# Adding the passes of an FFN projection onto x1's rows by DMA, under a stricter rule for fetching activation blocks

## The chip, the cores and the metric

The kernel runs on one core of a Trainium2 chip. The metric is the device time of one execution in microseconds (us).

## What is computed

One layer of a hybrid decoder on x of 512 tokens by 2048 features, in float32. Cut to what matters here:

```
h   = RMSNorm(x);  proj = h @ W_in                       # u, v_sgu, q, k, v_att, g_a, g_b
x1  = x  + (sigmoid(g_a) * (y_a @ W_up_a) + sigmoid(g_b) * (y_b @ W_up_b)) @ W_o
hid = silu(gate) * up,   [gate | up] = RMSNorm(x1) @ W_ffn_in       # 5632 wide
x2  = x1 + hid @ W_ffn_out                               # this product is the place of the change
out = x2 + sigmoid(RMSNorm(x2) @ W_pg) * (p @ W_ple)
```

y_a is a chunked spatial gating of u and v_sgu, y_b a stick-breaking attention. Activations lie transposed: features on the 128 partitions, tokens along the free axis. A block of 128 x 1024 holds two tiles of 128 features for all 512 tokens.

## The kernel before, in words

**Products.** Every float32 operand is split into a high part (ACT, a rounding copy to fp32r) and a low part (DVE, the difference), and a product is the sum of three matmuls (L284 to L286: high by high, high by low, low by high; L695 where two of them go as one). A unit is one 256 x 256 block of weights by one activation block. A unit of kind "S" goes by Strassen's seven products and needs seven blocks for each side; one of kind "P" goes plainly with four. The strings PASSES, GATE and OUT give each unit's kind.

**Weights.** SP loads a unit's weights (L327 plain; L329 and L331 for "S"). For "S", a DMA on POOL's queue then adds two blocks onto two others on the way (L351, accum_op=add), DVE adds two more sums (L363), ACT writes the high parts whi (L347) and DVE the low parts wlo (L344).

**Forms.** The activation side of a unit is a "form" in the SBUF arena `parts`, built from raw blocks in the arena `wholes` (128 x 13312 float32). A form of kind "S" is built in two halves: its block is loaded (L504), ACT and DVE split it (L274, L275) and the unit can be used plainly at once; later the block is loaded a second time with room for the Strassen sums, L513 forms these (after the gains of a norm, L508, where there are any), and L274 and L275 split them. `PLAIN_UNTIL` and `GATE_UNTIL` say for how many outputs of a stage a unit is still taken plainly while its second half is made.

**The clock that sets the order.** The program is written out in the order of a counter. After every few products `tick()` advances it by one; there are two ticks to an "S" pair of units. At each tick: (1) of the first three forms waiting in `builds` (AHEAD = 3), the first whose source has been written and for which there is room gets its block fetched; (2) the first form whose block was fetched WAIT = 2 ticks ago takes its first building step, or else one form of the queue `seconds` has its second block fetched; (3) what was put off by `after(n, ...)` and is due is issued. Every arena gives out its places by age: "old" takes the place that was given back the longest ago. What a tick issues is tied to its place among the matmuls on every engine.

**The stages.** In FFN-in, 44 outputs of hid are made and stored to DRAM as 22 blocks. The product with W_ffn_out runs over these 22 units in three passes of 8, 8 and 6 units, with eight outputs of 128 x 1024 each (`pair`, then `out` or `onto`):

- pass 0: each output is stored as a row block of `sum` (L1436, SP);
- pass 1: `sum` is loaded (L504), the output added onto it (L804 for outputs mixed from Strassen products, L808 for plain ones), and it is stored again (L1441);
- pass 2: `sum` and the row block of x1 are loaded, the output is added (L804), the whole is scaled by the norm's row (L1224), x1 is added (L1444), x2 stored (L1445), and its squares go to the third norm (L956, L960).

The scaling comes last because the norm's factor is one number for each token and so commutes with the product. The gate stage then builds its forms from the stored x2 rows with gains (L508) and finishes each output (L1455 on). Forms of the next stage are appended to `builds` before the last output of a stage, those of the gate stage before pass 2 begins.

Of the kernel before, what the change touches and what calls it, by code (L numbers as in the profile page):

```python
# [37 lines left out]

AHEAD, WAIT = 3, 2
PARTS = 16 * PLACE + 1024  # L40
# [27 lines left out]
def hybrid_layer(  # L68
# [44 lines left out]
    class Arena:  # L113
        def __init__(self, name, n, dt):
            self.tile, self.dt = keep.tile([P, n], dt, name=name), dt
            self.holes = [(0, n)]
            self.given, self.turns = np.zeros(n // P, int), 0

        def take(self, n, how="low"):


            spots = []
            for start, size in self.holes:
                end = start + size
# [10 lines left out]
            at = min(spots)[1]  # L135
            start, size = next(h for h in self.holes if h[0] <= at < h[0] + h[1])
            self.holes.remove((start, size))
            self.holes.extend(
                h for h in ((start, at - start), (at + n, start + size - at - n)) if h[1])
            return Block(self, at, n)  # L140

        def give(self, block):
            self.turns += 1
            self.given[block.start // P : -(-(block.start + block.n) // P)] = self.turns
            holes = sorted(self.holes + [(block.start, block.n)])
            self.holes = holes[:1]
            for s, n in holes[1:]:
# [40 lines left out]
    newest = {}  # L188
    builds, seconds = deque(), deque()

# [9 lines left out]
    def tick():  # L200

        clock[0] += 1
        last, units = traced()[-1], dict(newest)
        urgent = [f for f in seconds if f.used]
        sizes = []
        for f in list(builds)[: 0 if urgent else AHEAD]:
            sizes += [s for s in f.sizes if s[0] is parts]
            raw = [(wholes, 1024, "old")]
# [224 lines left out]
    class Form(Staged):  # L433


        def __init__(self, kind, steps, sizes, ready, src=None, far=False):
# [3 lines left out]
            self.src, self.there, self.block, self.due = src, not far, None, 0  # L440
            self.second, self.due_second, self.forced = None, 0, False

# [854 lines left out]
    ys = {(c, i): y_form(c, i) for c in "ba" for i in range(4)}  # L1297
    builds.extend(ys.values())
    for n, ((w, i), pr) in enumerate(zip(order, made())):
# [24 lines left out]
        else:  # L1324
# [9 lines left out]
          for j, k in enumerate(OUT) for how in [{} if k == "S" else {"how": "high"}]]  # L1334
    builds.extend(ms)
    for j in range(KU):
        for b in "ba":
# [14 lines left out]
            else:  # L1352
# [7 lines left out]
    norm2 = Norm()  # L1360
    spill = {(n, j): tc.dram_tile([P, 1024], F32, name=nm(n)) for n in ("x1", "sum", "x2")
             for j in range(KU)}
# [9 lines left out]
    for j in range(KU):  # L1372
        if j < KU - 1:
            raw.append(load(xT[j + 1]))
        if j == 1:
            ple_operands()
            builds.extend(fs)
        pr = pair(ms, last=j == KU - 1)
# [31 lines left out]
    for m in range(KH):  # L1410
        if m == KH - 1:
            builds.extend(hs[0])
        o = pair(fs, last=m == KH - 1, j=m, until=(1,) * KU, doubled=7).out()
# [10 lines left out]
    for c, units in enumerate(hs):  # L1424
        first, at = at, at + len(units)
        if c == len(hs) - 1:
            builds.extend(gs)
        for j in range(KU):
            if j == KU - 1 and c < len(hs) - 1:
                builds.extend(hs[c + 1])  # L1430
            before = load(spill["sum", j]) if c else None
            x1 = load(spill["x1", j]) if c == len(PASSES) - 1 else None
            pr = pair(units, last=j == KU - 1, j=j, until=PLAIN_UNTIL[c], at=first,
                      doubled=7)
            if before is None:
                nc.sync.dma_start(out=spill["sum", j], in_=pr.out())  # L1436
                continue
            h = before.f()
            pr.onto(h)
            if x1 is None:  # L1440
                nc.sync.dma_start(out=spill["sum", j], in_=h)  # L1441
            else:
                scaled(h, row2)
                nc.vector.tensor_tensor(out=h, in0=h, in1=x1.f(), op=ALU.add)  # L1444
# [122 lines left out]
```

## Time and profile before

| what | value |
|---|---|
| time, three executions | 2689.34, 2690.93, 2696.23 us; median 2690.93 |
| the profiled execution, its own time | 2691.74 us |
| its span in the trace | 2690.0 us |
| mean granted clock of TensorE | 0.998 |
| busy: PE, PEld, DVE, ACT, POOL | 2653.3, 2325.7, 2207.7, 1388.7, 458.2 us |
| pass 0 | 2058.0 to 2212.5 us of the span |
| pass 1 | 2212.5 to 2375.3 |
| pass 2 | 2375.3 to 2509.2 |
| gate stage | 2509.2 to 2690.0 |

PE is the TensorE matmul queue, PEld its weight loads, DVE VectorE, ACT ScalarE, POOL GpSimd and SP SyncE, which issues DMAs. L351 is line 351 of the kernel before. A row of PE's timeline gives the start, the length, the instruction, and in brackets how long the engine stood before it and what ended that. The span is what the trace covers of an execution, its own time is a little longer; the predicted time is set against the median.

### The profile page before, as it was taken

The page shows a single profiled execution, that of the slowest core. Times are in us where ns is not written, and L with a number is a line of the kernel's source. Part 1 is how long each engine was busy: PE and PEld are TensorE (multiplying, and loading weights), DVE is VectorE, ACT ScalarE, POOL GpSimd, SP SyncE. Part 2 cuts the span into 40 slices and gives each one's busy share as a digit, 9 for nine tenths or more (in the row PEclk, how much of TensorE's full clock was granted, in tenths as well). Part 3 has the DMA queues.
Part 4 walks back from the last instruction along what each step waited for, and adds up shares of the span by engine and source line. Part 5 has one row for each costly group of instructions (what it writes and reads, how often), then busy time and mean ns, then how long its engine had stood idle before and what let it go on. Part 6 is the DMA issues. An engine that isn't in the chain of part 4 may idle for free.

```text
span 2690.0 us, 42553 instructions
## 1 busy us (share of the span) xinstructions
PE 2653.3 (99%) x15496; PEld 2325.7 (86%) x15496; DVE 2207.7 (82%) x3715; ACT 1388.7 (52%) x2161; POOL 458.2 (17%) x549
## 2 busy tenths in 40 slices
PE   8999999999999999999999999999999999999999
PEld 7889898889898889988888888888888888888898
DVE  8687878787887666688898888888899889889876
ACT  7656565655554334375444444444445444444543
POOL 0223323232220000001111111111110111100010
PEclk9999999999999999999999999999999999999999
DMA  7677777777776457667888888888888979978884
GB/s 226 154 185 175 182 173 184 172 183 198 174 187 196 140 164 211 178 210 198 230 212 213 204 202 200 201 206 199 207 197 244 259 213 279 259 254 259 257 248 126
DMA packets 288241, 548.62 MB, mean 204 GB/s; under 512 B 25888, under 2 KB 138272, under 8 KB 288032
## 3 DMA queue, kind: packets, MB, share of 16 engines
q1 hardware_dynamic: 229232, 441.03, 50.3%
q0 software_dynamic: 58800, 104.88, 25.2%
q8 instruction: 121, 1.98, 0.3%
q14 instruction: 88, 0.72, 0.1%
HBM read 498.63 MB, written 47.19 MB: 203 GB/s over the span
## 4 chain that ended last, share of the span: by engine, by line
PE 85%; DVE 7%; DMA 3%; ACT 2%; issue 2%; POOL 1%; SPq 0%; DVEq 0%; ACTq 0%; POOLq 0%
PE ps L695 47%; PE ps L285 10%; PE ps L286 10%; PE ps L284 10%; PE small L695 6%; DVE wlo L344 2%; DVE out L754 1%; DMA wholes<-x 1%; DVE parts L275 1%; PE small L1157 1%; DMA wholes<-hid 1%; DVE wholes L363 1%; ACT whi L347 1%; DVE wholes L513 1%; PE small L1032 1%
## 5 line engine op out<-in xcount | busy, mean ns | idle before, releaser
L695 PE MATMUL ps<-parts,whi 128*128 128x512 f32 x3960 | 1324.8, 397 | 0.3 <-DVE p L754 0.3
L347 ACT ACTIVATE whi<-wholes 128x512 fp32r<-128x512 f32 (+3 forms) x933 | 866.0, 942 | 787.0 <-DVE wholes L363 274.0
L344 DVE TENSOR_TENSOR wlo<-wholes,whi 128x512 fp32r<-128x512 f32 (+3 forms) x933 | 974.1, 1078 | 85.6 <-ACT whi L347 85.4
L695 PEld LDWEIGHTS ps<-parts,wlo 128*128 128x128 f32 x3960 | 743.7, 188 | 168.1 <-issue 1.0
L695 PE MATMUL ps<-parts,wlo 128*128 128x256 f32 x3960 | 784.3, 279 | 0.1
L285 PE MATMUL ps<-parts,whi 128*128 128x256 f32 (+1 forms) x2070 | 679.5, 329 | 4.8 <-DVE parts L275 4.7
L284 PE MATMUL ps<-parts,whi 128*128 128x256 f32 (+1 forms) x2048 | 668.1, 328 | 12.4 <-ACT parts L274 10.6
L286 PE MATMUL ps<-parts,wlo 128*128 128x256 f32 (+1 forms) x2070 | 677.6, 329 | 1.7 <-DVE wlo L344 1.7
L695 PEld LDWEIGHTS ps<-parts,whi 128*128 128x128 f32 x3960 | 637.8, 189 | 5.9 <-issue 1.0
L285 PEld LDWEIGHTS ps<-parts,whi 128*128 128x128 f32 x2070 | 393.6, 190 | 46.5 <-DVE parts L275 7.3
L284 PEld LDWEIGHTS ps<-parts,whi 128*128 128x128 f32 x2048 | 388.5, 190 | 48.9 <-ACT parts L274 12.7
L286 PEld LDWEIGHTS ps<-parts,wlo 128*128 128x128 f32 x2070 | 393.5, 190 | 36.2 <-DVE wlo L344 3.2
L363 DVE TENSOR_TENSOR wholes<-wholes 128x256 f32<-128x256 f32 (+1 forms) x806 | 338.9, 420 | 19.1 <-issue 1.7
L754 DVE TENSOR_TENSOR out<-out,ps 128x256 f32<-128x256 f32 x460 | 190.8, 417 | 150.9 <-ACT out L751 150.2
L351 POOL DMA_DIRECT2D wholes<-w_ffn_in x172 | 150.1, 872 | 689.1 <-DVE wholes L363 251.7
L351 POOL DMA_DIRECT2D wholes<-w_in x132 | 118.3, 898 | 484.4 <-DMA wholes<-w_in 133.7
L695 PE MATMUL small<-parts,whi 128*128 128x512 f32 x440 | 174.5, 397 | 0.0
L275 DVE TENSOR_TENSOR parts<-wholes,parts 128x1024 fp32r<-128x1024 f32 (+4 forms) x134 | 131.0, 989 | 17.6 <-ACT parts L274 17.6
L274 ACT ACTIVATE parts<-wholes 128x1024 fp32r<-128x1024 f32 (+4 forms) x134 | 112.9, 865 | 46.9 <-DVE wholes L513 26.1
L351 POOL DMA_DIRECT2D wholes<-w_ffn_out x64 | 55.8, 872 | 402.5 <-DMA wholes<-w_ffn_out 101.6
L751 ACT ACTIVATE out<-ps 128x256 f32<-128x256 f32 x243 | 91.4, 385 | 47.5 <-PE ps L695 44.0
L1403 ACT ACTIVATE out<-out 128x512 f32<-128x512 f32 x44 | 27.9, 633 | 156.3 <-DVE out L1402 156.3
(120 smaller groups left out, 1721.6 us busy)
## 6 DMA issues: line engine op xcount, KB each, us to landing
wholes<-w_ffn_in SPq DMA_DIRECT2D x172, 384.0 KB, 5.6
wholes<-w_in SPq DMA_DIRECT2D x132, 384.0 KB, 5.0
wholes<-w_ffn_in SPq DMA_DIRECT2D x172, 256.0 KB, 4.8
wholes<-w_ffn_in POOLq DMA_DIRECT2D x172, 256.0 KB, 5.5
wholes<-w_in SPq DMA_DIRECT2D x132, 256.0 KB, 4.2
wholes<-w_in POOLq DMA_DIRECT2D x132, 256.0 KB, 4.9
wholes<-w_ffn_out SPq DMA_DIRECT2D x64, 384.0 KB, 5.4
wholes<-hid SPq DMA_DIRECT2D x42, 512.0 KB, 5.8
```

Of the source, the lines that this page charges most:

```text
L274: return (nc.scalar.activation(hi, src, AF.Copy), nc.vector.tensor_tensor(out=lo, in0=src, in1=hi.bitcast(F32), op=ALU.subtract))
L275: nc.vector.tensor_tensor(out=lo, in0=src, in1=hi.bitcast(F32), op=ALU.subtract))
L284: nc.tensor.matmul(ps, sh, mh, start=start, stop=False)
L285: nc.tensor.matmul(ps, sh, ml, start=False, stop=False)
L286: return nc.tensor.matmul(ps, sl, mh, start=False, stop=stop)
L344: in_turn(nc.vector.tensor_tensor(out=self.lo[:, blocks], in0=r, in1=h.bitcast(F32), op=ALU.subtract))
L347: in_turn(nc.scalar.activation(h, r, AF.Copy))
L351: nc.gpsimd.dma_start(out=raw[:, 3:5], in_=self.src[:, 1:3], accum_op=ALU.add)
L363: in_turn(nc.vector.tensor_tensor(out=o, in0=x, in1=y, op=ALU.add))
L695: m = nc.tensor.matmul(out, l, r, start=first and k == 0, stop=last and k == 1)
L751: in_turn(nc.scalar.activation(out, x, AF.Copy, scale=scale))
L754: in_turn(nc.vector.tensor_tensor(out=out, in0=x, in1=y, op=op))
```

## The change

Three things change; everything up to the last output of FFN-in is issued as before. Lines of helpers move down by 17 (L504 becomes L521, L351 becomes L368, L513 becomes L530).

- Each pass's output is scaled by the norm's row at once (24 times instead of 8). Passes 0 and 1 put off, by two ticks, a DMA on POOL's queue that adds the output onto x1's row block in DRAM. The tensor `sum` with its 16 stores and 16 loads is gone. Pass 2 loads only x1's row block, adds its output, and stores x2 one tick later.
- A block is fetched only into a place of `wholes` that was given back at least REST = 2 ticks ago (`rested`). The same holds for second halves.
- Forms carry the number of their stage; while a form of an earlier stage still waits for its second block, no block of a later stage is fetched.

```diff
-AHEAD, WAIT = 3, 2
+AHEAD, WAIT, REST = 3, 2, 2
@@ Arena
-            self.given, self.turns = np.zeros(n // P, int), 0
-
-        def take(self, n, how="low"):
+            self.given, self.when = np.zeros(n // P, int), [0]
+
+        def spots(self, n, how):
             spots = []
...
+            return spots
+
+        def rested(self, n):
+            spots = self.spots(n, "old")
+            return bool(spots) and clock[0] - self.when[min(spots)[0]] >= REST
+
+        def take(self, n, how="low"):
+            at = min(self.spots(n, how))[1]
...
         def give(self, block):
-            self.turns += 1
-            self.given[block.start // P : -(-(block.start + block.n) // P)] = self.turns
+            self.given[block.start // P : -(-(block.start + block.n) // P)] = len(self.when)
+            self.when.append(clock[0])
@@ tick
+        stage = min((f.stage for f in seconds), default=1 << 30)
         sizes = []
         for f in list(builds)[: 0 if urgent else AHEAD]:
+            if f.stage > stage or not wholes.rested(1024):
+                break
             sizes += [s for s in f.sizes if s[0] is parts]
...
-        elif seconds and fits([(wholes, 5 * 256, "old")]):
+        elif seconds and fits([(wholes, 5 * 256, "old")]) and wholes.rested(5 * 256):
             (urgent or seconds)[0].fetch_second()
@@ the three passes
-            before = load(spill["sum", j]) if c else None
-            x1 = load(spill["x1", j]) if c == len(PASSES) - 1 else None
+            end = c == len(hs) - 1
+            h = load(spill["x1", j]) if end else None
             pr = pair(units, last=j == KU - 1, j=j, until=PLAIN_UNTIL[c], at=first,
                       doubled=7)
-            if before is None:
-                nc.sync.dma_start(out=spill["sum", j], in_=pr.out())
+            o = pr.out()
+            scaled(o, row2)
+            if not end:
+                after(2, lambda o=o, j=j: nc.gpsimd.dma_start(
+                    out=spill["x1", j], in_=o, accum_op=ALU.add))
                 continue
-            h = before.f()
-            pr.onto(h)
-            if x1 is None:
-                nc.sync.dma_start(out=spill["sum", j], in_=h)
-            else:
-                scaled(h, row2)
-                nc.vector.tensor_tensor(out=h, in0=h, in1=x1.f(), op=ALU.add)
-                nc.sync.dma_start(out=spill["x2", j], in_=h)
+            nc.vector.tensor_tensor(out=h.f(), in0=h.f(), in1=o, op=ALU.add)
+            norm3.add(h)
+
+            def store(h=h, j=j):
+                nc.sync.dma_start(out=spill["x2", j], in_=h.f())
                 there.add(("x2", j))
-                norm3.add(before)
-                give(x1)
-            give(before)
+                give(h)
+
+            after(1, store)
```

Each list of forms gets its stage number by `build(forms)`, which takes the place of `builds.extend(forms)`. On POOL's queue, 64 accumulates of w_ffn_out stand in a row before; afterwards the 16 accumulates onto x1 stand among them, one after every one to five.

**The first place** is on SP, at the step from pass 0 to pass 1. The hid rows are the activation blocks; those of pass 1 are numbered 10836 to 10843 in the kernel before. The sum rows belong to outputs, w_ffn_out to weights.

```order
L504 DMA wholes<-hid_10836 128x1024
L329 DMA wholes<-w_ffn_out 128x2x256
L331 DMA wholes<-w_ffn_out 128x768
L504 DMA wholes<-sum_9218 128x1024
L329 DMA wholes<-w_ffn_out 128x2x256
L331 DMA wholes<-w_ffn_out 128x768
L1436 DMA sum_9225<-out_20054 128x1024
L327 DMA wholes<-w_ffn_out 128x1024
L504 DMA wholes<-hid_10842 128x1024
L504 DMA wholes<-hid_10837 128x1024
L327 DMA wholes<-w_ffn_out 128x1024
L504 DMA wholes<-hid_10843 128x1024
```

The same place after the change, where the blocks of pass 1 are numbered 10828 to 10835:

```order
L346 DMA wholes<-w_ffn_out 128x2x256
L348 DMA wholes<-w_ffn_out 128x768
L521 DMA wholes<-hid_10834 128x1024
L521 DMA wholes<-hid_10835 128x1024
L521 DMA wholes<-hid_10828 128x1024
L346 DMA wholes<-w_ffn_out 128x2x256
L348 DMA wholes<-w_ffn_out 128x768
L344 DMA wholes<-w_ffn_out 128x1024
L521 DMA wholes<-hid_10829 128x1024
L344 DMA wholes<-w_ffn_out 128x1024
L521 DMA wholes<-hid_10830 128x1024
L521 DMA wholes<-hid_10831 128x1024
```

The seventh and eighth first blocks (10842 and 10843 before, 10834 and 10835 after) stood behind second halves and a sum load and store; now they stand ahead of every second half.

**The second place** is on SP, at the step from pass 1 to pass 2, whose blocks are 10844 to 10849 before. First the kernel before:

```order
L504 DMA wholes<-hid_10847 128x1024
L327 DMA wholes<-w_ffn_out 128x1024 x2
L504 DMA wholes<-hid_10848 128x1024
L504 DMA wholes<-sum_9218 128x1024
L327 DMA wholes<-w_ffn_out 128x1024
L329 DMA wholes<-w_ffn_out 128x2x256
L331 DMA wholes<-w_ffn_out 128x768
L504 DMA wholes<-x_823_9210 128x1024
L1441 DMA sum_9225<-wholes 128x1024
L329 DMA wholes<-w_ffn_out 128x2x256
L331 DMA wholes<-w_ffn_out 128x768
L504 DMA wholes<-hid_10849 128x1024
```

After the change, with blocks 10836 to 10841 in pass 2 (x_823 and x_824 are x1's first two row blocks):

```order
L344 DMA wholes<-w_ffn_out 128x1024 x5
L521 DMA wholes<-hid_10840 128x1024
L521 DMA wholes<-x_823_9210 128x1024
L344 DMA wholes<-w_ffn_out 128x1024
L346 DMA wholes<-w_ffn_out 128x2x256
L348 DMA wholes<-w_ffn_out 128x768
L521 DMA wholes<-hid_10841 128x1024
L521 DMA wholes<-hid_10837 128x1024
L521 DMA wholes<-x_824_9211 128x1024
L346 DMA wholes<-w_ffn_out 128x2x256
L348 DMA wholes<-w_ffn_out 128x768
L521 DMA wholes<-hid_10838 128x1024
```

The first blocks of units 1 to 4 (10836 to 10839) are no longer here: they stand early in pass 1, with the second block of the first unit. The sum rows are gone.

**The third place** is on DVE at the same step, in the last output of pass 1, just ahead of the split of the first second half. Before:

```order
L754 TENSOR_TENSOR p_1786_21489<-p_1786_21489,ps_21389 128x256
L754 TENSOR_TENSOR out_21484<-out_21484,ps_21395 128x256
L754 TENSOR_TENSOR out_21484<-out_21484,p_1786_21489 128x2x256
L754 TENSOR_TENSOR out_21484<-out_21484,ps_21395 128x256
L754 TENSOR_TENSOR out_21484<-ps_21400,out_21484 128x256
L754 TENSOR_TENSOR out_21484<-small_21405,out_21484 128x256
L754 TENSOR_TENSOR out_21484<-out_21484,ps_21400 128x256
L754 TENSOR_TENSOR out_21484<-out_21484,small_21405 128x256
L344 TENSOR_TENSOR wlo_79<-wholes,whi_78 128x1024
L275 TENSOR_TENSOR parts<-wholes,parts 128x4x256
```

After:

```order
L530 TENSOR_TENSOR wholes<-wholes 128x256 x3
L771 TENSOR_TENSOR out_21476<-out_21476,ps_21385 128x256
L530 TENSOR_TENSOR wholes<-wholes 128x256
L771 TENSOR_TENSOR out_21476<-out_21476,p_1802_21481 128x2x256
L771 TENSOR_TENSOR out_21476<-out_21476,ps_21385 128x256
L771 TENSOR_TENSOR out_21476<-ps_21390,out_21476 128x256
L771 TENSOR_TENSOR out_21476<-small_21395,out_21476 128x256
L771 TENSOR_TENSOR out_21476<-out_21476,ps_21390 128x256
L771 TENSOR_TENSOR out_21476<-out_21476,small_21395 128x256
L361 TENSOR_TENSOR wlo_79<-wholes,whi_78 128x1024
L292 TENSOR_TENSOR parts<-wholes,parts 128x4x256
```

Four additions of the first unit's Strassen sums (L530) now stand among the mixing of the output (L771, L754 before), ahead of the split.

More of the change, by code (lines that the diff above doesn't have):

```diff
@@ L134, in take @@
                                      for a in {*range(start, end - n + 1, 256), end - n})
-            at = min(spots)[1]
+            return spots
[4 more added lines that the diff above has]
+            at = min(self.spots(n, how))[1]
             start, size = next(h for h in self.holes if h[0] <= at < h[0] + h[1])
@@ L188, in hybrid_layer, with build @@
     newest = {}
-    builds, seconds = deque(), deque()
+    builds, seconds, stages = deque(), deque(), iter(range(1 << 30))
+    def build(forms):
+        stage = next(stages)
+        for f in forms:
+            f.stage = stage
+        builds.extend(forms)
     def mark(instruction):
@@ L440, in __init__ @@
             self.src, self.there, self.block, self.due = src, not far, None, 0
-            self.second, self.due_second, self.forced = None, 0, False
+            self.second, self.due_second, self.forced, self.stage = None, 0, False, -1
         def fetch(self):
@@ L1297, in hybrid_layer @@
     ys = {(c, i): y_form(c, i) for c in "ba" for i in range(4)}
-    builds.extend(ys.values())
+    build(ys.values())
     for n, ((w, i), pr) in enumerate(zip(order, made())):
@@ L1334, in hybrid_layer @@
           for j, k in enumerate(OUT) for how in [{} if k == "S" else {"how": "high"}]]
-    builds.extend(ms)
+    build(ms)
     for j in range(KU):
@@ L1360, in hybrid_layer @@
     norm2 = Norm()
-    spill = {(n, j): tc.dram_tile([P, 1024], F32, name=nm(n)) for n in ("x1", "sum", "x2")
+    spill = {(n, j): tc.dram_tile([P, 1024], F32, name=nm(n)) for n in ("x1", "x2")
              for j in range(KU)}
@@ L1376, in hybrid_layer @@
             ple_operands()
-            builds.extend(fs)
+            build(fs)
         pr = pair(ms, last=j == KU - 1)
@@ L1411, in hybrid_layer @@
         if m == KH - 1:
-            builds.extend(hs[0])
+            build(hs[0])
         o = pair(fs, last=m == KH - 1, j=m, until=(1,) * KU, doubled=7).out()
```

4 lines of the change are left out of this document (2 added, 2 removed).

## The prediction

> **What bounds the kernel now.** I read first the page's busy times and the chain that ended last, then the four stages that the change can reach (pass 0, pass 1, pass 2 and the gate stage) as four windows, then PE's waits in them, and last the instructions ahead of each wait.
>
> ```profile
> span 2690.0 us, 42553 instructions
> PE 2653.3 (99%) x15496; PEld 2325.7 (86%) x15496; DVE 2207.7 (82%) x3715; ACT 1388.7 (52%) x2161; POOL 458.2 (17%) x549
> PE 85%; DVE 7%; DMA 3%; ACT 2%; issue 2%; POOL 1%; SPq 0%; DVEq 0%; ACTq 0%; POOLq 0%
> ```
>
> PE is busy for 99% of the span and holds 85% of the chain. Its matmuls are the same 15378 program rows before and after, so a gain can only come out of the time in which PE stands or runs slowly. The stages, with the columns window, length, PE, PEld, DVE, ACT, POOL, PE's clock, DMA share, GB/s:
>
> ```profile
> 2058.00:2212.50 154.50, 154.49 (x876) 134.43 (x875) 136.67 (x238) 77.94 (x104) 21.82 (x25) 1.00 0.86 248
> 2212.50:2375.30 162.80, 160.85 (x902) 139.40 (x901) 148.15 (x252) 78.81 (x105) 21.80 (x25) 1.00 0.90 263
> 2375.30:2509.20 133.90, 127.31 (x790) 114.38 (x789) 116.06 (x169) 61.47 (x77) 10.47 (x12) 0.99 0.83 258
> 2509.20:2690.00 180.80, 172.75 (x1097) 157.40 (x1095) 134.29 (x205) 81.88 (x109) 19.93 (x20) 0.99 0.71 209
> ```
>
> Pass 0 has no PE idle time to win; pass 1 has 1.95 us, pass 2 6.59, and the gate stage 8.05 (the kernel's tail with its last stores among it). PE's timeline names each pause: start, length, and in brackets the idle time before and its releaser.
>
> ```profile
> 2228.89 0.50 PE L285 MATMUL ps<-parts,whi 128*128 128x512 f32 x1 [1.25 <-DVE parts L275]
> 2242.52 0.62 PE L284 MATMUL ps<-parts,whi 128*128 128x256 f32 x3 [0.64 <-ACT parts L274]
> 2390.92 0.73 PE L284 MATMUL ps<-parts,whi 128*128 128x512 f32 x2 [1.52 <-ACT parts L274]
> 2419.66 0.62 PE L284 MATMUL ps<-parts,whi 128*128 128x256 f32 x3 [2.04 <-ACT parts L274]
> 2421.31 0.39 PE L285 MATMUL ps<-parts,whi 128*128 128x256 f32 x1 [0.32 <-DVE parts L275]
> 2423.33 0.62 PE L284 MATMUL ps<-parts,whi 128*128 128x256 f32 x3 [1.05 <-ACT parts L274]
> 2424.59 0.39 PE L285 MATMUL ps<-parts,whi 128*128 128x256 f32 x1 [0.64 <-DVE parts L275]
> 2463.22 0.39 PE L286 MATMUL ps<-parts,wlo 128*128 128x256 f32 x1 [1.02 <-DVE wlo L344]
> 2528.03 0.80 PE L944 MATMUL small<-diag,ones 128*128 128x128 f32 x4 [0.76 <-DVE diag L942]
> 2564.13 0.39 PE L285 MATMUL ps<-parts,whi 128*128 128x256 f32 x1 [2.00 <-DVE parts L275]
> ```
>
> Together 11.24 us. Eight of the ten wait for L274 or L275, the split of a form: the first products of a stage wait for an activation block that was fetched or split late. Two windows in which the clock fell follow right behind the largest groups of them:
>
> ```profile
> 2425.30:2428.70 3.40, 3.40 (x15) 3.11 (x14) 2.91 (x5) 3.10 (x5) 0.00 (x0) 0.50 0.90 336
> 2565.30:2568.70 3.40, 3.40 (x18) 3.40 (x17) 3.40 (x4) 0.26 (x1) 0.00 (x0) 0.50 0.82 243
> ```
>
> Half a clock for 3.40 us loses 1.7 us, so 3.4 us in both. No more than 11.24 + 3.4 = 14.6 us can be won, 0.5%.
>
> Here a rule of the Trainium skill can be weighed. Its page "TensorE: Matmul & The Clock Gate", section "HAM oscillation — how this bites in real kernels", says that PE must not idle for more than about 3.4 us; by it pauses of 2.0 us would leave the clock alone, and the 3.4 us would stay whatever becomes of them. The trace does not agree: the longest single pause before either window is 2.04 or 2.00 us.
>
> **What the change costs and brings, part by part.** *Where the forms are fetched* (first and second place of the order). Before, SP issued the blocks of the next stage among sum loads and stores, and one of them was seen to hold ACT up:
>
> ```profile
> 2215.39 2.47 SPq L504 DMA_DIRECT2D wholes<-hid  x2
> 2219.87 1.46 SPq L504 DMA_DIRECT2D wholes<-hid  x2
> 2389.81 1.06 ACT L274 ACTIVATE parts<-wholes 128x1024 fp32r<-128x1024 f32 x1 [3.11 <-DMA wholes<-hid]
> ```
>
> In pass 1 the first of each of those SP pairs is the seventh and the eighth block of the stage; they came 13.5 and 9.0 us before the pause at 2228.89. In the changed order they stand 53 to 60 matmuls earlier, ahead of every second half; a matmul of that stage is 160.85/902 = 0.18 us, so some 10 us. The 1.25 us go. In pass 2 the first blocks of units 1 to 4 are fetched early in pass 1, and of the stage's end only units 5 and 6, the second halves and two x1 rows are left; the sum loads that stood between are gone. I take the five pauses from 2390.92 to 2424.59 away: 1.52 + 2.04 + 0.32 + 1.05 + 0.64 = 5.57 us, and the clock window behind them, 1.7. In the gate stage the late block's split is now ordered 76 matmuls ahead of its reader: 2.00 and 1.7 us go. The pause of 0.64 stays, since the second half of pass 1's second form is again split about ten matmuls ahead of its use; I add another 0.64 for the same pattern one form earlier. The 0.76 us stay: L942 is not touched.
>
> *DVE.* What its operations take:
>
> ```profile
> L804 DVE TENSOR_TENSOR wholes<-wholes,out 128x1024 f32<-128x1024 f32 x13 | 15.9, 1220 | 0.0
> L1224 DVE TENSOR_TENSOR wholes<-wholes 128x1024 f32<-128x1024 f32 x8 | 9.8, 1220 | 0.1
> L1444 DVE TENSOR_TENSOR wholes<-wholes 128x1024 f32<-128x1024 f32 x8 | 9.8, 1222 | 0.1
> L513 DVE TENSOR_TENSOR wholes<-wholes 128x256 f32<-128x256 f32 x78 | 30.9, 419 | 5.3 <-ACT wholes L508 2.8 <-DMA wholes<-hid 2.3
> ```
>
> Pass 0 gains eight scalings, 8 x 1.22 = 9.8 us: DVE goes from 136.67 to about 146 of 154.5. Its cover is that pass 1 already runs at 148.15 of 162.8 with the same count of such operations for each output, and no pause of it comes from wlo or from the mixing of outputs. I count 0; without that cover it would be at most 9.8. Pass 1 trades an addition for a scaling: 0. Pass 2 loses eight operations of 1.22 us. There the pause of 1.02 us at 2463.22 came when L344 stood behind L804, L1224 and L1444 of one pair, 3.7 us; with 1.2 us less in the row it goes. The new cost stands at the third place of the order: four additions (30.9/78 = 0.40 us each, 1.6 together) now go ahead of a split that PE reads one matmul later. PE waits between 0 and the largest pause of the kind, 2.0; I take 1.0, the middle, which is near the 1.25 and 1.05 above.
>
> *The new store of x2, one tick later.* A tick here is 2.8 us (133.9 us of pass 2 over 8 pairs of 6 ticks). The rows of x2 made earlier have that to spare; the last two go store, load, gain, split, PE, with 42 to 44 matmuls (7.5 us) from load to reader. Bounds 0 and 2.8 us, a whole tick: I take 1.0, by the same rows. Nothing is queued behind these waits on ACT that PE needs sooner.
>
> *DMA.* 32 plain transfers of 512 KB go (16 stores and 16 loads of sum) and 16 accumulates of 512 KB come, on POOL's queue.
>
> ```profile
> q1 hardware_dynamic: 60552, 132.04, 60.7%
> q0 software_dynamic: 12539, 20.64, 20.9%
> wholes<-w_ffn_out POOLq DMA_DIRECT2D x62, 256.0 KB, 5.7
> wholes<-sum SPq DMA_DIRECT2D x16, 512.0 KB, 5.4
> sum<-out SPq DMA_DIRECT2D x8, 512.0 KB, 3.4
> ```
>
> Of the 632 us of this window the plain queue took 383.6 for 132.04 MB, 1.52 us of all 16 engines for each 0.524 MB; the accumulating one 132.1 for 20.64 MB, 3.36. So 32 x 1.52 = 49 us go and 16 x 3.36 = 54 come: even. No trace row shows an accumulate into DRAM; its landing lies between 3.4 (a plain store) and twice 5.7 (two accumulates into SBUF). Nobody waits for it: x1's row is read a pass later, and the out buffer is wanted again two pairs on (154.5/8 = 19.3 us a pair). On POOL it costs one issue, in a queue busy for 22 of 160 us. I count 0; the other end is the first rival.
>
> **The sum.** Gone: 1.25 + 5.57 + 1.7 + 1.02 + 2.00 + 1.7 = 13.2 us. New: 0.64 + 1.0 + 1.0 = 2.6. Net 10.6 us less. The profiled span of 2690.0 becomes 2679.4 and its own time 2691.74 becomes 2681.1; that execution lay 0.8 above the median of 2690.93, which becomes 2680.3. I say **2680.5**.
>
> **Rivals.** *The weights come late (slower).* Each accumulate onto x1 stands on POOL's queue among the accumulates that finish the Strassen weights, which PE needs. Of those in pass 1, from issue to landing, and ACT's wait for them in passes 0 and 1:
>
> ```profile
> DMA to landing us min/median/max: 4.2/6.0/9.0
> ACT whi L347 <- DMA wholes<-w_ffn_out: 11.4, 5, 4.6
> ```
>
> Against it: landings up to 3.0 us over the median happened, ACT idled for them five times, and no PE pause in those passes waits for whi or wlo. For it: if a weight's sum lands a whole transfer, 3.36 us, later on top of these, and cover is about 2 us, each of 16 accumulates would stop PE for some 1.4 to 1.6 us, +22 to +26 us; less the 10.6 won, **2702 to 2706**. It decides once the delay passes about 2 us at most accumulates; at 0.7 us each the gain is just used up. The Trainium skill's page "DMA: Bandwidth & Descriptors", section "Queues, rings and completion order", says that an engine consumes the descriptors of one ring in order. By that rule a weight's accumulate issued right behind would wait for all of x1's, and this rival would be the outcome where their issues lie within some 3 us.
>
> *Waits move instead of going (same).* A block may now be fetched only into a place that has rested for two ticks, and only for the stage at hand. Where that holds a load past its reader, the removed pauses come back under another name; with half of the 7.57 us at the starts of pass 2 and of the gate stage back (3.8), and one clock window with them (1.7), the gain is 10.6 - 5.5 = 5.1: **2685.8**. For it: the changed order still has three splits within seven matmuls of their reader.
>
> *The clock windows stay (same).* They also occur elsewhere; without the 3.4 us the gain is 7.2: **2683.7**.
>
> *The change does nothing PE can see*, since sums and x1 weigh the same on DMA: 2690, within the two cases above in sign.
>
> **Chances.** "Same" is within 0.3%, 8.1 us, about what a measurement of this kernel can tell: from 2682.9 to 2699.0. Forecast 0.45; waits moved 0.18; clock windows stay 0.08; nothing seen 0.07; weights late 0.22. So faster 0.45, same 0.33, slower 0.22. The low end takes the forecast without its 2.6 us of new terms and 3 us more where the order runs freer, 2675; the high end reaches into the first rival, 2703, and leaves the worst of it, about 0.15, and 0.05 below. The likeliest case alone spans 2675 to 2683.
>
> **What would show it.** Right: PE's waits from 2058 on fall from 11.2 to about 4 us, none of 1.5 us or more for L292 or L291 (the new lines of L275 and L274) remains behind pass 2's and the gate's start, and the two half-clock windows are gone. DVE's share of pass 0 rises by 9 to 10 us and PE stays unbroken there. The first rival would show as PE waits for whi or wlo in passes 0 and 1, behind a POOL landing over 9 us. The second would show hid or x2 loads issued under 10 us before their reader. My forecast is wrong if the accumulate delays other transfers of the same engines more than its 3.36 us say, or if DVE in pass 0 has less slack than pass 1 promised.

## The result, and the profile after

| kernel | median us | executions | against before (95% interval) |
|---|---|---|---|
| before | 2690.95 | 4, 2689.34 to 2696.23 | |
| after the change | 2679.00 | 4, 2675.77 to 2681.47 | 0.9954 [0.9942, 0.9966] |

The change takes 11.95 us off, 0.44%; 10.4 were forecast, from 2690.93 to 2680.5. The profiled execution after the change took 2681.47 us, its slowest of four, with a span of 2679.8. Some of that is chance: it reached pass 0 2.8 us later than the profiled execution before, in a part of the program that the change does not touch. From pass 0 on it is 13.0 us shorter.

First the page after, then its four stages cut at the matmuls that stood at the cuts before (window, length, PE, PEld, DVE, ACT, POOL, PE's clock, DMA share, GB/s):

```profile
span 2679.8 us, 42579 instructions
PE 2650.4 (99%) x15496; PEld 2323.7 (87%) x15496; DVE 2206.0 (82%) x3716; ACT 1392.4 (52%) x2169; POOL 467.4 (17%) x565
```

```profile
2061.00:2216.70 155.70, 154.69 (x875) 134.24 (x874) 143.84 (x246) 78.19 (x104) 28.15 (x32) 1.00 0.92 249
2216.70:2377.90 161.20, 160.55 (x901) 139.16 (x900) 148.45 (x250) 79.41 (x105) 28.91 (x33) 1.00 0.91 240
2377.90:2503.70 125.80, 124.82 (x790) 112.92 (x789) 111.79 (x167) 66.36 (x87) 11.38 (x13) 1.00 0.81 246
2503.70:2679.80 176.10, 170.65 (x1097) 155.48 (x1095) 129.72 (x202) 79.27 (x106) 20.05 (x20) 1.00 0.71 208
```

Length less PE is PE's idle time: 1.0, 0.65, 1.0 and 5.5 us, 8.1 together, where it was 16.6. Pass 2 is 8 us shorter, the gate stage nearly 5; pass 0 has become a little longer. PE's waits from 2050 us on, and the rows of its timeline in which they stand:

```profile
PE ps L712 <- DVE wlo L361: 1.5, 2, 0.9
PE ps L301 <- ACT whi L364: 0.5, 1, 0.5
PE ps L303 <- DVE wlo L361: 0.5, 2, 0.3
```

```profile
2104.82 0.50 PE L712 MATMUL ps<-parts,wlo 128*128 128x256 f32 x2 [0.87 <-DVE wlo L361]
2266.22 0.50 PE L712 MATMUL ps<-parts,wlo 128*128 128x256 f32 x2 [0.64 <-DVE wlo L361]
2382.23 0.50 PE L301 MATMUL ps<-parts,whi 128*128 128x512 f32 x1 [0.52 <-ACT whi L364]
2386.33 0.50 PE L303 MATMUL ps<-parts,wlo 128*128 128x512 f32 x1 [0.18 <-DVE wlo L361]
2457.09 0.39 PE L303 MATMUL ps<-parts,wlo 128*128 128x256 f32 x1 [0.28 <-DVE wlo L361]
```

2.5 us are left of 11.2, and not one of them waits for a form (L291, L292). Both half-clock windows that the prediction named are gone. What the DMA queues did from 2061 to 2680:

```profile
q1 hardware_dynamic: 55967, 115.36, 54.0%
q0 software_dynamic: 14759, 28.86, 29.0%
wholes<-w_ffn_out POOLq DMA_DIRECT2D x62, 256.0 KB, 5.3
x<-out POOLq DMA_DIRECT2D x16, 512.0 KB, 8.3
```

The shares of both queues add up to 83.0% of 619 us, 514 us of all 16 engines; before they were 60.7 + 20.9 = 81.6% of 632 us, 516 us. The weights' accumulates land no later (5.3 us, 5.7 before).

### The profile page after: what moved, and what is told of

The parts are those of the page before. It is cut to its first block, busy times and chain, and to the rows that moved or that the text cites. A ratio compares the mean times of both kernels' runs of the same rounds, so it can differ in the third digit from the quotient of the medians.

```text
span 2679.8 us, 42579 instructions
## 1 busy us (share of the span) xinstructions
PE 2650.4 (99%) x15496; PEld 2323.7 (87%) x15496; DVE 2206.0 (82%) x3716; ACT 1392.4 (52%) x2169; POOL 467.4 (17%) x565
## 4 chain that ended last, share of the span: by engine, by line
PE 87%; DVE 6%; DMA 2%; ACT 2%; issue 2%; POOL 1%; SPq 0%; DVEq 0%; ACTq 0%; POOLq 0%
PE ps L712 48%; PE ps L303 11%; PE ps L302 11%; PE ps L301 10%; PE small L712 6%; DVE wlo L361 2%; DVE out L771 1%; PE small L1174 1%; DMA wholes<-x 1%; DVE wholes L380 1%; DVE parts L292 1%; PE small L1049 1%; DVE wholes L530 1%; ACT whi L364 1%; PE small L1124 0%
## 5 line engine op out<-in xcount | busy, mean ns | idle before, releaser
L361 DVE TENSOR_TENSOR wlo<-wholes,whi 128x512 fp32r<-128x512 f32 (+3 forms) x933 | 974.8, 1079 | 82.2 <-ACT whi L364 81.5
L380 DVE TENSOR_TENSOR wholes<-wholes 128x256 f32<-128x256 f32 (+1 forms) x806 | 338.8, 420 | 19.3 <-DVE wlo L361 1.7
L771 DVE TENSOR_TENSOR out<-out,ps 128x256 f32<-128x256 f32 x460 | 190.6, 416 | 144.0 <-ACT out L768 143.6
L368 POOL DMA_DIRECT2D wholes<-w_ffn_in x172 | 150.0, 872 | 689.7 <-DVE wholes L380 216.4
L368 POOL DMA_DIRECT2D wholes<-w_in x132 | 118.2, 897 | 490.9 <-DMA wholes<-w_in 135.4
L292 DVE TENSOR_TENSOR parts<-wholes,parts 128x1024 fp32r<-128x1024 f32 (+4 forms) x136 | 131.2, 977 | 18.1 <-ACT parts L291 18.0
L291 ACT ACTIVATE parts<-wholes 128x1024 fp32r<-128x1024 f32 (+4 forms) x136 | 112.6, 854 | 43.1 <-DVE wholes L530 22.7
L368 POOL DMA_DIRECT2D wholes<-w_ffn_out x64 | 55.9, 873 | 360.7 <-DVE wholes L380 66.1
```

The source lines that it names most:

```text
L291: return (nc.scalar.activation(hi, src, AF.Copy), nc.vector.tensor_tensor(out=lo, in0=src, in1=hi.bitcast(F32), op=ALU.subtract))
L292: nc.vector.tensor_tensor(out=lo, in0=src, in1=hi.bitcast(F32), op=ALU.subtract))
L361: in_turn(nc.vector.tensor_tensor(out=self.lo[:, blocks], in0=r, in1=h.bitcast(F32), op=ALU.subtract))
L368: nc.gpsimd.dma_start(out=raw[:, 3:5], in_=self.src[:, 1:3], accum_op=ALU.add)
L380: in_turn(nc.vector.tensor_tensor(out=o, in0=x, in1=y, op=ALU.add))
L771: in_turn(nc.vector.tensor_tensor(out=out, in0=x, in1=y, op=op))
```

## The experiments

All of them are read the same way: which PE waits come back. Kernels 1 to 4, 5 to 8 and 9 to 12 ran on three chips; each is set against the runs of the kernel before on its own chip. The ratios are estimated from all executions and so differ a little from those of the medians. "Alone" below is the kernel of the first experiment.

| kernel | median us | before, same chip | against before (95%) |
|---|---|---|---|
| 1 accumulates alone | 2676.63 | 2691.37 | 0.9949 [0.9937, 0.9962] |
| 2 fetch rules alone | 2698.82 | 2691.37 | 1.0025 [1.0012, 1.0038] |
| 3 no rest | 2679.11 | 2691.37 | 0.9952 [0.9939, 0.9964] |
| 4 store at once | 2679.26 | 2691.37 | 0.9958 [0.9944, 0.9971] |
| 5 alone, places held | 2683.13 | 2690.45 | 0.9974 [0.9963, 0.9985] |
| 6 + loads | 2689.32 | 2690.45 | 0.9992 [0.9983, 1.0002] |
| 7 + loads and stores | 2694.06 | 2690.45 | 1.0011 [1.0002, 1.0020] |
| 8 whole, accumulates doubled | 2689.34 | 2690.45 | 0.9994 [0.9985, 1.0003] |
| 9 alone, accumulates left out | 2678.94 | 2691.59 | 0.9952 [0.9940, 0.9964] |
| 10 the whole change again | 2679.22 | 2691.59 | 0.9955 [0.9943, 0.9967] |
| 11 accumulates alone again | 2678.39 | 2691.59 | 0.9956 [0.9943, 0.9968] |
| 12 alone + stores | 2679.65 | 2691.59 | 0.9958 [0.9946, 0.9970] |

Set matmul against matmul with the trace of before, the stages of the profiled executions changed by the following (us; one execution each, so that 1 or 2 us of a cell can be chance; what lies ahead of pass 0 differs by -4.0 to +2.8 us and is left out):

| kernel | pass 0 | pass 1 | pass 2 | gate stage |
|---|---|---|---|---|
| after | +1.2 | -1.5 | -8.1 | -4.7 |
| 1 accumulates alone | +0.1 | -2.7 | -7.4 | -0.2 |
| 2 fetch rules alone | +0.4 | +2.7 | -1.8 | +8.9 |
| 3 no rest | +0.1 | -2.6 | -3.1 | -4.3 |
| 4 store at once | +2.7 | -1.5 | -8.4 | -3.3 |
| 5 alone, places held | +1.4 | +1.9 | -6.9 | -4.7 |
| 6 + loads | +1.9 | +9.0 | -5.5 | -4.7 |
| 7 + loads and stores | +1.5 | +9.6 | -4.2 | -4.8 |
| 8 whole, doubled | +3.5 | -0.1 | -6.2 | -4.8 |
| 9 accumulates left out | +0.1 | -2.7 | -8.5 | -2.3 |
| 11 accumulates alone again | +0.1 | -2.3 | -7.4 | -2.6 |
| 12 alone + stores | +1.2 | -2.5 | -7.2 | -2.2 |

**1. The accumulates alone.**

```diff
-AHEAD, WAIT, REST = 3, 2, 2
+AHEAD, WAIT, REST = 3, 2, 0
-            if f.stage > stage or not wholes.rested(1024):
+            if not wholes.rested(1024):
-            after(1, store)
+            store()
```

> Only the first part of the change: sum is replaced by accumulates onto x1, with the fetch rules of before (no rest, no stage numbers) and x2 stored at once. Theory A (late forms: the time won is the pauses of PE for forms that came late, and whatever part fetches them earlier wins it): in this order the fifth and sixth block of pass 2 are loaded 21 and 28 matmuls ahead of their reader (39 for the later one with the whole change, 21 for the one that cost 1.52 us before), all others 37 or more; so one pause of 1 to 2 us comes back at the start of pass 2, and the time is 2680 to 2682. Theory B (the fetch rules carry the gain, the accumulates only trade traffic): over half of the gain is lost, 2685 or more. Theory C (traffic: what wins is that 32 transfers of sum are gone): the same as the whole change, 2679.

Measured: 14.7 us faster than before, all of the gain. So theory B falls: the fetch rules carry none of it. Theory C's number, 2679, lies nearest. The pause that theory A expected at the start of pass 2 did not come either: a block loaded 21 matmuls ahead of its reader was in time. PE's waits of this kernel from 2050 us on:

```profile
PE small L961 <- DVE diag L959: 2.5, 1, 2.5
PE ps L303 <- DVE wlo L361: 0.8, 1, 0.8
PE ps L301 <- ACT whi L364: 0.5, 1, 0.5
PE ps L302 <- DVE parts L292: 0.3, 1, 0.3
```

What it waits for and the whole change does not is the first row, the norm's chain at the start of the gate stage; a half-clock window of 3.41 us follows it, at 2518.47. The trace accounts for less than 14.7 us: pauses fell from 11.2 to 4.2 us and two windows became one, 8.7 us in all, and the four stages add up to 10.2. The repeat of this kernel (11) was 13.2 us faster than before, so some us of the lead are chance.

**2. The fetch rules alone**, with the passes over `sum` as before.

> Only the fetch rules (rest of two ticks, stage numbers); the passes go over sum as before, x2 stored at once. Theory A (late forms): the pause of 1.25 us at the start of pass 1 goes, since its blocks are fetched earlier; at the start of pass 2 one second half is still loaded only 29 matmuls ahead of its reader and the gate's blocks 39 to 48 ahead, so some 2 to 4 us of the 5.57 there and part of the 2.00 stay: 2684 to 2688. Theory B (the rules carry it): 2679 to 2682. Theory C (traffic): 2691, no change.

Measured: 7.5 us slower than before, outside every theory's number. The profiled execution was the slowest of its six (2703.58 us), so its pauses add up to more than that. The three longest on PE, the clock behind the second, and ACT's rows behind the second and third:

```profile
2426.95 0.62 PE L301 MATMUL ps<-parts,whi 128*128 128x256 f32 x3 [3.25 <-ACT parts L291]
2526.22 0.38 PE L301 MATMUL ps<-parts,whi 128*128 128x256 f32 x1 [2.97 <-ACT whi L364]
2577.95 1.22 PE L301 MATMUL ps<-parts,whi 128*128 128x256 f32 x4 [3.83 <-ACT parts L291]
```

```profile
2526.80:2536.80 10.00, 9.46 (x43) 8.95 (x42) 6.38 (x12) 6.08 (x9) 2.35 (x2) 0.50 0.81 277
```

```profile
2524.89 1.27 ACT L364 ACTIVATE whi<-wholes 128x1280 fp32r<-128x1280 f32 x1 [5.60 <-DMA wholes<-w_gate]
2569.87 0.72 ACT L525 ACTIVATE wholes<-wholes,gcol 128x512 f32<-128x512 f32 x1 [5.95 <-DMA wholes<-x]
```

In the gate stage a block of x2 comes so late that ACT idles 5.95 us for it and PE 3.83 after it; the pause of 2.97 us is for a block of w_gate, a weight, and 10.24 us at half clock follow it. That rested places are too few while the sum blocks and x1's sit in `wholes` may be the reason. It is not shown, and no run took the two rules apart there. This is the rival "waits move instead of going", and it is true of the rules, though not of the change.

**3 and 4. The change without one rule each**: REST = 0, and `store()` instead of `after(1, store)`.

> The whole change without the rest of two ticks (REST = 0); stage numbers and the later store stay. Theory A (late forms): its loads at the starts of passes 1 and 2 stand as in the kernel with the accumulates alone (21 and 28 matmuls ahead of the reader in pass 2), so a pause of 1 to 2 us and 2680 to 2682. Theory B: over 2685. Theory C: 2679.

> The whole change, but x2's rows are stored at once instead of a tick later. My prediction charged the later store 1.0 us (0 to 2.8): by it this runs at 2678, with 0 charged at 2679. Rival: the later store keeps SP's queue from standing behind DVE (SP waits in order for the store's data, and loads queued behind it wait too), so that storing at once costs a load its lead; then 2680 to 2682, with a pause at the start of the gate stage.

Measured: 2679.11 and 2679.26, both as the whole change. In the written program the stage numbers decide nothing where REST is 0 (the third kernel is row for row the first with the later store), so the runs 1 and 3 differ by the later store alone, as do 4 and the whole change. Medians of executions that scatter by several us cannot settle a charge of 1.0 us. The waits speak against the charge: with x2 stored at once, as in the fourth kernel, the gate stage starts with a pause that the whole change does not have, the one that the expectation's rival named:

```profile
2516.98 0.71 PE L961 MATMUL small<-diag,ones 128*128 128x128 f32 x4 [1.34 <-DVE diag L959]
```

The third kernel has 0.34 us there, and 2.48 us for wlo in pass 2 with a half-clock window behind it, at a matmul where the others wait 0.8 at most. So its time equals that of the whole change by another set of waits.

**5. Places held** (in the accumulates alone).

```diff
+            held = take(1024, "old") if c else None
             h = load(spill["x1", j]) if end else None
...
             scaled(o, row2)
+            if c:
+                give(held)
```

> The accumulates alone (the first run of the study, 2676.6), and a place of 1024 columns of wholes is taken before each pair of passes 1 and 2 and given back after its output, as the sum block was: no load, no store, no work. Theory P (places: a sum block that sits in wholes for a whole pair keeps the blocks of forms from being fetched): the two last first blocks of pass 1 stand again 46 and 43 matmuls ahead of their reader (44 and 39 with sum), and the pause of 1 us or so at the start of pass 1 comes back: 2679 to 2682, and 2685 or more if the places are the main cause. Theory C (traffic and SP's queue): 2676.6, no change.

Measured: 2683.13, between the two numbers of theory P; theory C's 2676.6 falls. 0.9974 stands against 0.9949 and 0.9956 without the held place, so 5 to 7 us of the gain go when nothing but a place in `wholes` is occupied. The intervals leave this uncertain by some 4 us. PE's timeline at the start of pass 1 has pauses of the kind and size that the expectation named:

```profile
2228.23 0.50 PE L302 MATMUL ps<-parts,whi 128*128 128x512 f32 x1 [0.71 <-DVE parts L292]
2232.93 0.39 PE L302 MATMUL ps<-parts,whi 128*128 128x256 f32 x1 [1.06 <-DVE parts L292]
```

Pass 1 is 4 us longer than without the held place. Pass 2 waits 2.3 us for forms, but stays 6.9 us shorter than before, and the gate stage 4.7. A pause of 0.62 us in the middle of pass 0, where no place is held yet, is hardly the place's doing; the runs 4, 6, 7, 8 and 12 have it as well.

**6 and 7. Loads into the held places, and stores besides.**

```diff
-            held = take(1024, "old") if c else None
+            held = load(spill["x1", j]) if c else None
...
             scaled(o, row2)
+            if not end:                                       # the seventh only
+                nc.sync.dma_start(out=spill["sum", j], in_=o)
```

> As the run with the place held, but a row block of x1 is loaded into the place (16 loads of 512 KB on SP, whose data nobody reads), as the sum blocks were. Theory P: no more than the held places cost, within 1.5 us. Theory C (traffic): half of the gain of 14.7 us is lost, 2682 to 2686, since 8 MB of the 16 MB are back.

> As the run with the dummy loads, and SP also stores each output of passes 0 and 1 into a scratch tensor as soon as DVE has scaled it (16 stores of 512 KB), beside the accumulates onto x1. Places, transfers and SP's queue are then those of the kernel before, plus the accumulates. Theory C (traffic): all of the gain is lost and more, 2690 to 2695. Theory P: as with the held places, 2678 to 2682. A third outcome, 2683 to 2687 with pauses for L291 or L292 at the starts of stages, says that loads queued on SP behind a store that waits for DVE come late (theory Q, SP's queue).

Measured: 2689.32 and 2694.06. The loads cost 6.2 us more than the held places, the stores 4.7 more. In SP's queue only four loads of forms stand elsewhere than in the fifth kernel, first blocks of pass 2 that are hundreds of matmuls ahead of their readers in both. With all of `sum`'s places and transfers back the kernel is 3.6 us slower than before. Theory P's numbers fall in both, theory Q's in the second. Theory C has the second (2690 to 2695) and misses the first (2682 to 2686) by 3 us, since it had no price for the places. The kernel with the loads shows one event in pass 1, on DVE, PE and the clock:

```profile
2300.43 0.89 DVE L380 TENSOR_TENSOR wholes<-wholes 128x256 f32<-128x256 f32 x2 [2.54 <-issue]
```

```profile
2302.56 0.79 PE L712 MATMUL ps<-parts,whi 128*128 128x512 f32 x1 [4.09 <-DVE out L771]
```

```profile
2300.90:2307.70 6.80, 5.14 (x16) 4.47 (x17) 5.96 (x13) 3.76 (x7) 1.48 (x2) 0.50 1.00 257
```

A weight's accumulate, issued at 2293.66, landed at 2300.35. DVE's next row, L380, needs it; L771, which frees the PSUM bank that PE wants, stands behind L380. PE loses 4.09 us, and 2.6 more, half of the 5.2 us that the clock stayed low after the pause. ACT took up five of the weights' accumulates in a row there 0.16 us after landing, and the DMA engines were busy all the time (share 1.00): the rival "the weights come late". The accumulate at 2293.66 did not stand behind one onto x1 (the next of those was issued at 2294.29). The kernel with loads and stores pauses at the same matmul, with 6.83 us at half clock behind it:

```profile
2298.33 0.50 PE L712 MATMUL ps<-parts,whi 128*128 128x512 f32 x1 [1.99 <-DVE out L771]
```

**8. Accumulates doubled.**

```diff
-                after(2, lambda o=o, j=j: nc.gpsimd.dma_start(
-                    out=spill["x1", j], in_=o, accum_op=ALU.add))
+                for n in ("x1", "x1b"):
+                    after(2, lambda o=o, j=j, n=n: nc.gpsimd.dma_start(
+                        out=spill[n, j], in_=o, accum_op=ALU.add))
```

> The whole change with every accumulate issued twice, the second onto a scratch copy of x1 (32 accumulates, 8 MB more on POOL's queue; the copy costs 8 stores much earlier). The prediction's slower rival (weights come late behind the accumulates): 16 more delays; if a transfer of 3.4 us eats the cover of the weights' sums, PE waits for whi or wlo in passes 0 and 1 and the time is 2690 to 2705. If there is cover for one accumulate and not for two, 2682 to 2688. My reading of the profile after (cover of 0.2 to 5 us at ACT, but PE hardly waits): 2679 to 2683.

Measured: 2689.34; 0.9994 against 0.9954 for the whole change, some 10.7 us. That lies between the two slower expectations, 1.3 us above the one of cover for one accumulate and not for two, and 0.7 us below the other. The author's own reading, 2679 to 2683, falls. ACT's waits for the weights' sums in passes 0 and 1 after the change, and then with two accumulates:

```profile
ACT whi L364 <- DMA wholes<-w_ffn_out: 14.3, 7, 3.6
```

```profile
ACT whi L364 <- DMA wholes<-w_ffn_out: 49.8, 19, 6.2
```

19 waits instead of 7; the other kernels with one set have 5 to 13, that without accumulates 5. The delay can be seen singly after the change, too: weights' accumulates issued 3.2, 3.9, 3.8 and 5.0 us behind one onto x1 landed after 8.2, 7.8, 7.2 and 7.8 us, against the median of 5.3. The prediction's sentence from the Trainium skill's page "DMA: Bandwidth & Descriptors", section "Queues, rings and completion order", points the same way. The cover, which the prediction put at about 2 us and no run measured, was there for one set and not for two. The profiled execution (2685.47) was one of the fastest of this kernel; what the median of 2689.34 lost beyond it is not in a trace.

**9 to 12. The cost of the first set, and the rules again.**

> The accumulates alone (as in the first run), but with the 16 accumulates left out: the outputs of passes 0 and 1 are scaled and dropped, so x2 lacks them; everything else stands as it was. What the accumulates themselves cost is the difference to the next kernel but one of this job. My sum charged them 0: the same time within 1.5 us. The doubled accumulates cost some 10 us more than single ones; if the first set costs as much as the second, this runs 8 to 11 us faster, about 2667.

```diff
             if not end:
-                after(2, lambda o=o, j=j: nc.gpsimd.dma_start(
-                    out=spill["x1", j], in_=o, accum_op=ALU.add))
                 continue
```

> The whole change again, on the same chip as the accumulates alone. If the rest of two ticks costs what the single profiles show (pass 0 took 1.2 to 2.7 us longer in the two kernels with it, 0.1 in the two without), it is 1 to 3 us slower than the accumulates alone; if those were chance, the two agree within 1 us.

> The accumulates alone again: 2675 to 2679, and not slower than the whole change. It is the better of the two if it leads by over 1 us here as well.

> The accumulates alone, and SP also stores each output of passes 0 and 1 into a scratch tensor when DVE has scaled it (16 stores of 512 KB); no place is held and nothing is loaded. Traffic theory: the held places cost about 6 us, loads on top 6 more, stores on top 5 more; if each adds by itself, this is 3 to 6 us over the accumulates alone. If the weights' sums are late only when the queues are fuller than this (loads and stores together), 0 to 2 us.

Measured: 2678.94 without accumulates, 2679.22 the whole change, 2678.39 the accumulates alone, 2679.65 with stores alone. The first 16 accumulates cost nothing that shows; the second 16 cost 10.7 us. Without any accumulate the two queues keep the engines busy for 76.4% of the stretch instead of 83%, and the time is the same. The lead of the accumulates alone over the whole change, 0.8 us here, is not clear: the same kernel gave 2676.63 on another chip, and whether it is the better one stays open. In pass 0 the pause of 0.87 us for L361, quoted first, stands in all four profiles with the accumulates and the rest (after, 4, 8, 10) and in none of the others. On the other side the kernels that store x2 at once wait 1.3 to 2.5 us for L959 at the start of the gate stage (1, 4, 9, 11, 12; not 2 and 5 to 7), and the ones that store later 0.3 at most. That the two cancel is a reading of these sums, not a run of its own. Stores alone cost 1.3 us, against 4.7 on top of the loads, as the second half of the expectation had it: places, loads and stores do not simply add.

## Why the prediction was right, and where it was off

**The bound.** PE's pauses and the clock windows behind them, at most 14.6 us, were the right account. 11.2 us of pauses became 2.5, and both windows went: 8.7 + 3.4 = 12.1 us, where 11.95 were measured.

**The starts of passes 1 and 2** (1.25 and 5.57 + 1.7). Gone, all six pauses. The prediction read this from where the loads stood in the order, among fewer sum loads, and did not say which of the edits put them there. The runs do: dropping `sum`. The rest of two ticks and the stage numbers, the larger part of the diff, contribute nothing in this kernel and cost 7.5 us in the kernel with `sum`.

What it is in `sum` that cost the time is shown only in part. A place held for a whole pair costs 5 to 7 us, most of it in pass 1, and the loads and stores on top bring back the rest, again most of it in pass 1 as far as single profiles show. The total of the transfers is not the cause: the accumulates put back on the engines what `sum` took off (514 us after, 516 before). With places, loads and stores all back, pass 2 still is 4.2 us shorter than before, though it waits 3.6 us for forms, and the gate stage 4.8. No run tells what removed that part of the pauses; the eight additions of 1.22 us that DVE no longer makes in pass 2, and the order that follows from them, are among what is left as a cause, untested.

**New waits** (0.64 + 0.64 kept + 1.0 + 1.0 + 0.76 kept = 4.0 us). Over-sized: after the change PE has 2.5 us of pauses. Behind the four additions PE stood 0.52 and 0.18 us, for whi and wlo and not for the split; neither a pause of 0.64 for a split nor the norm's 0.76 came; the later store shows no cost. Two pauses that were charged 0, 0.87 us in pass 0 and 0.64 in pass 1, came instead, both for wlo. Pass 1's DVE load was to be the cover, and it held for the scaling: without the rest pass 0 is unchanged (+0.1 us in the runs 1, 3, 9 and 11) though DVE works off the same scalings. Both pauses came with the rest of two ticks: the third kernel, without it, has neither. (The kernels 5 to 7 and 12 lose 1.2 to 1.9 us in pass 0, with pauses for L771 and not for wlo.) So two of the signs that the prediction named failed: PE did not stay unbroken in pass 0, and DVE rose by 7.2 us there and not by 9 to 10 (143.84 against 136.67; seven of the eight scalings fall into the window). That the forecast came within 1.5 us owes something to luck: waits that did not come were charged where others came uncharged.

**wlo in pass 2** (1.02). Gone in the main; 0.28 and 0.18 are left.

**The gate stage** (2.00 + 1.7). Gone, and here 3.95 us of the difference stand in one stretch, 2545 to 2570 of before, in every kernel but the second. The kernels 5 to 7 are among them, so neither the place nor the transfers of `sum` had caused it. The prediction's reason, that the late block's split moved ahead of its reader, fits this; which edit moved it was not tried by itself.

**DMA "even", accumulates at 0.** Right: 516 us of all 16 engines before, 514 after. The plain queue lost 49 us, as forecast, and the accumulating one gained 47 of the 54, 3.0 us for each accumulate instead of 3.36. An accumulate of 512 KB onto DRAM landed, from issue, in these times (min, median, max), and took POOL a little longer to issue than the 0.87 us of a weight's:

```profile
L1455 POOL DMA_DIRECT2D x<-out x16: 875/1167/1201, 2082.8 to 2384.7; - x16
```

```profile
DMA to landing us min/median/max: 5.2/8.3/9.6
```

8.3 us lies between the bounds of 3.4 and 11.4. But 0 is the price of the trade, not of an accumulate: the room comes from the 32 transfers that left. Where they stay (7), or where a second set comes (8), the slower rival happens, in a milder form than its price of 2702 to 2706: 2694 and 2689, by way of L380 and L771 on DVE.

**The clock windows.** The rival that they stay fell for this stretch. That 2.0 us can be enough to set one off is right, for the window in the gate stage; the one in pass 2 began 5.7 us behind the pause of 2.04, after three more (2.04 + 0.32 + 1.05 + 0.64 = 4.05 us of pauses together). That such a pause must set one off is not right, as the last section shows.

## What to carry to other kernels

When PE is busy 99% of the time, list its pauses with what follows each on the clock: their sum is all there is to win. A partial sum that travels through SBUF costs more than its DMA: the place it holds keeps other loads from being issued, and here that alone was worth 5 to 7 of some 14 us. An accumulate on the queue that also finishes the weights is free only while the engines have room, so count what leaves before what comes; and try each edit of such a change by itself, since one that reads like the main part may do nothing, or harm.

## What was not expected of the hardware

A pause of PE well under a window's length can halve the clock, but need not. Over the fourteen profiles, after the first 10 us, none of the 29 pauses from 1.2 to 1.7 us had a window at half clock begin within 2 us of its end, 8 of the 25 from 1.75 to 2.38 us had, and 8 of the 10 from 2.45 to 4.09 us had one, begun in the pause or behind it. This one of 2.45 us, in the kernel with doubled accumulates, left the clock whole, as the window behind it shows:

```profile
1197.11 0.49 PE L961 MATMUL small<-diag,ones 128*128 128x128 f32 x2 [2.45 <-DVE diag L959]
```

```profile
1197.10:1200.50 3.40, 3.39 (x17) 2.87 (x18) 1.15 (x4) 1.16 (x2) 0.89 (x1) 1.00 1.08 332
```

This one of 2.48 us, in the kernel without the rest, did not:

```profile
2437.75 0.58 PE L303 MATMUL ps<-parts,wlo 128*128 128x256 f32 x1 [2.48 <-DVE wlo L361]
```

```profile
2437.70:2441.10 3.40, 3.35 (x15) 3.35 (x16) 3.33 (x9) 0.45 (x1) 0.00 (x0) 0.50 0.90 270
```

Inside the program the windows are 3.41 us long or a multiple of it (6.83 at the pause of 4.09 and behind that of 1.99, 10.24 behind that of 2.97), so a pause that sets one off costs PE some 1.7 to 5.1 us beyond itself, and near 2 us it goes either way in one and the same kernel. The section "HAM oscillation — how this bites in real kernels" of the Trainium skill's page "TensorE: Matmul & The Clock Gate" sets the limit at about 3.4 us; these runs show half clock after pauses shorter than that, down to 1.75 us.
